# Hybrid decoder trunk: the sigmoid's table loaded early, the first low part behind the root, the third joint unit's first raw sum on VectorE, and the reloads of x two joint units later

## The chip, the cores and the metric

The kernel runs on one core of a Trainium2 chip. The metric is the device time of one execution in microseconds (us); where several runs are given, it is their median. The engines are called PE (matmuls), DVE (VectorE), ACT (ScalarE), POOL (GpSimd) and SP (SyncE, which here only starts DMAs).

## The reference

The trunk has two residual layers on a sequence of 1024 positions by 1024 channels, all in float32. Each layer is a token mixer and a SwiGLU network, each behind an RMSNorm and a modulation by a conditioning vector c:

```python
c_act = silu(c)
for i in range(2):
    sh_m, sc_m, g_m, sh_f, sc_f, g_f = split(c_act @ ada_w[i] + ada_b[i], 6)
    h = rms_norm(x, norm_mix_g[i]) * (1 + sc_m) + sh_m
    y = conformer_conv(h, ...) if i == 0 else multiscale_pool(h, ...)
    x = x + (1 + g_m) * y
    h = rms_norm(x, norm_ffn_g[i]) * (1 + sc_f) + sh_f
    x = x + (1 + g_f) * ((silu(h @ w_gate[i]) * (h @ w_up[i])) @ w_down[i])
return rms_norm(x, final_g)

def conformer_conv(h, ...):
    a, g = split(h @ w1 + b1, 2)
    u = a * sigmoid(g)
    u = silu(layer_norm(causal_depthwise_conv(u, width=31)))
    return u @ w2 + b2
```

The pooling mixer of layer 1 takes trailing means of 2, 4, 8 and 16 positions in four groups of channels, less the token itself, and maps each group linearly. The inner width of the SwiGLU network is 2816.

## The kernel before

**Number format.** A float32 product is made of three PE products in the type fp32r: each operand is split into a high part (a cast) and a low part (the operand less its high part), and high x high, high x low and low x high are summed. A weight tile `raw` (128 x 1024) thus costs a DMA (L473 in `load_weight`, L469), an ACT cast to the high part of `w`, and a subtraction on DVE or POOL for the low part, `w<-raw,w` in the profile. Activations are split in the same way into `h` high (ACT) and `h` low (DVE).

**Tiling.** Channels lie on the 128 partitions, in 8 tiles of channels. The sequence is cut into two chunks of 512 positions, A and B, so that a matmul is 128 x 128 by 128 x 512. Every engine's instruction is recorded at L122, a matmul at L144, and many of SP's DMAs at L154.

**Order of the work.** PE's order is written by hand: the order of the code. The other engines' orders come from a scheduler that works with estimated prices; where it would choose wrongly, the code ties an instruction behind another by an edge that is only an order and no semaphore (`add_manual_dep(..., edge, ...)`). `V_`, `S_` and `G_` issue on DVE, ACT and POOL. `either(n)` picks DVE or POOL.

**First stage (L1450 to L1525).** Chunk A's sums of squares go through PE; DVE works out the reciprocal root of their means in some ten small steps on 128 x 4 (`var`, `col`, in `rsqrt`, L496), and PE spreads it over the partitions (`rstd<-ident,col`). Beside it DVE multiplies tiles of the modulation weights by silu(c) and sums them (`ada_dot`; `adaw<-adaw,cact`), which gives shift and scale. Then for each of 8 channel tiles k, `t` is the normed and scaled x (DVE), `h` its split, and PE multiplies 8 banks (`first`) with weight tile k: 24 products a tile. The first two weight tiles' low parts are DVE's own (`own=k < 2`). When the last tile is through, ACT makes the sigmoid of the gate banks (`t<-first,vecs`), and the convolution's stage follows: the rest of the first matrix (`a`, `g`), the taps on DVE, POOL and ACT, and further modulation vectors by PE (`ada<-adaw,ccols`), whose weights come by SP (`adaw<-in_adan_dram`). ACT holds one function table at a time; its change is the row ACT_TABLE_LOAD.

**Joint units (L1080 to L1230, layer by layer).** In the SwiGLU network chunk A's first products are made ahead, and the two chunks' remaining products are put together by Strassen-like combinations: `joint(l, fp)` takes, for each of 11 pairs of inner channels `fp`, four quarters w0 to w3 of the gate and up weights and makes five weight tiles from sums of them, by `joint_weights`:

- `s2`: s = w0 + w3, and `s1`: w2, for the parts t2 (PE bank `a`) and t1 (PE bank `e`),
- `s3`: w0, `s4`: w1 + s (`raw<-raw,s` in the profile), `a22`: w3, for the parts n3 (`a`), b22 (`e`) and n4 (`a`).

Ahead of that, the quarters themselves are sums: `added(i, src)` (L1091) adds a quarter from memory onto a loaded one by an accumulating DMA of POOL's queue. For every fp but 0, w0 += w2 comes first and then w2 += w3. In layer 0's second unit (fp 1) the first of the two is a DVE addition instead. The name `raw<-in_wgu_dram` stands for loads and accumulations alike, `s<-raw,raw` for the sum s. When t1 is done, DVE takes the bank's two halves away by `t<-e,r`, and b22 writes into the same bank (`e<-b,w`), so PE waits for these two instructions. DVE prepares the next unit's weights while PE works on this one: `s<-raw,raw` and `t<-e,r` of two neighbouring units stand in one queue.

**Reloads.** The residual x of chunk A was stored to memory (`xd`) before and is taken back in four blocks during the joint units by `x_in(A, m)` (L331), an SP DMA `x<-xd` tied behind the last matmul of a unit. `all_joint` (L1648) runs the 11 units.

Of the kernel before, what the change touches and what calls it, by code (L numbers as in the profile page):

```python
# [9 lines left out]
F32 = mybir.dt.float32  # L10
# [6 lines left out]
P = 128  # L17
# [110 lines left out]
def trunk(ctx, tc, xT, c, vec, ada, adan, w1f, w1, wdg, w2, wgu, wdn, wpl, out):  # L128
# [232 lines left out]
    def V(name, j, n=1):  # L361
        b = _COLS[name] + j
        return vecs[:, b : b + n]
# [9 lines left out]
    def ada_dot(w, l, j, k):  # L373
        b = (l * 6 + j) * KT + k
        V_.scalar_tensor_tensor(w, w, 1.0, cact, op0=MUL, op1=MUL, accum_out=mod[:, b : b + 1])
# [711 lines left out]
    def joint_weights(l, fp):  # L1087

        w = {}

        def added(i, src):  # L1091
            d = order(nc.gpsimd.dma_start(w[i], wgu[l, fp, src], accum_op=ADD))  # L1092
            if fp == 1:
                st["added"].append(d.ins)
            clock["G"] = max(clock["G"], clock["PE"]) + 0.9

        def loads():
            for i in (0, 3, 2, 1) if fp else (2, 0, 3, 1):
                w[i] = quarter(l, fp, i, "u1")
            if fp == 1 and l == 0:  # L1100
                V_.tensor_tensor(w[0], w[0], w[2], op=ADD)
                if st["third"]:
                    tc.add_manual_dep(V_.last.ins, st["third"], edge, reason="behind the combinations")
                else:
                    st["early"].append(V_.last.ins)
            else:
                added(*((0, 2) if fp else (2, 3)))
            added(*((2, 3) if fp else (0, 2)))

        def later():  # L1110

            if fp == 1 and st["read"]:
                tc.add_manual_dep(V_.last.ins, st["read"], edge, reason="behind the first unit's reads")
            elif fp == 1:
                st["next"].append(V_.last.ins)

        def s2():
            if fp:
                loads()
            w[4] = block("u0", "s2", F32).rearrange("p a b -> p (a b)")  # L1120
            either(D).tensor_tensor(w[4], w[0], w[3], op=ADD)
            later()
            wt = combined(w[4])
            later()
            return wt

        def s1():
            if fp == 0:
                loads()
            wt = combined(w[2], fp == 0)  # L1130
            if fp:
                later()
            return wt

        def s3():
            wt = combined(w[0], fp == 0, True)
            later()
            return wt

        def s4():  # L1140
            either(D).tensor_tensor(w[1], w[1], w[4], op=ADD)
            return combined(w[1])

        def a22():
            wt = combined(w[3], fp == 0 and l == 0, True, wgu[l, fp, 3])
            if fp == 0 and l == 0:
                return wt
            if fp == 0 and st["third"]:
                tc.add_manual_dep(V_.last.ins, st["third"], edge, reason="behind the combinations")
            elif fp == 0:  # L1150
                st["early"].append(V_.last.ins)
            return wt

        return s2, s1, s3, s4, a22
# [319 lines left out]
    V_.scalar_tensor_tensor(acc, squares[KT - 1], EPS_SUM, acc, op0=ADD, op1=ADD)  # L1474
    summed = V_.last.ins.name
    S_.activation(ccols[:, :, 0], V("c", 0, KT), AF.Silu)
    scale_b = cst.tile([P, KT], F32, name="scale_b")
    G_.tensor_scalar(scale_b, V("ada_b", KT, KT), 1.0, None, op0=ADD)
    ada_m = ada.rearrange("(l j k) p d -> l k p j d", l=DEPTH, j=6)
# [14 lines left out]
    for k in range(KT + 1):  # L1494
# [14 lines left out]
                products(fb[q], wt, q, h_a[k - 1], k == 1, k == KT)  # L1509
        if k < KT:  # L1510
            ada_dot(w[:, 0], 0, 0, k)
            tc.add_manual_dep(V_.last.ins, low_last if k else rstd_last, edge, reason="behind the first norm")
            if k == 1:
                tc.add_manual_dep(dots[0], low_last, edge, reason="behind the first values")
            V_.tensor_scalar(scale_m[:, k : k + 1], mod[:, KT + k : KT + k + 1], scale_b[:, k : k + 1], V("norm_mix_g", k), op0=ADD, op1=MUL)
            V_.tensor_scalar(mod[:, k : k + 1], mod[:, k : k + 1], V("ada_b", k), None, op0=ADD)
            t = temp(A.n) if k else first_t
            V_.scalar_tensor_tensor(t, x[0][k], scale_m[:, k : k + 1], rstd_a if k else rstd_p, op0=MUL, op1=MUL)
            t_last = V_.last.ins.name
            S_.activation(h_a[k][0], t, AF.Identity, bias=mod[:, k : k + 1])  # L1520
            if k == 0:
                rstd_a = temp(A.n, "ny", 2)
                S_.copy(rstd_a, rstd_p)
            wt = load_weight(w1f[k], 2 * FIRST * P, load_next, own=k < 2)
    st["T"] = {}  # L1525
    for e in clock:
        clock[e] = max(clock.values())
# [123 lines left out]
    def all_joint(l, n, first=None, behind_it=None):  # L1651
# [6 lines left out]
        rest = [2 * q for q in range(ROUNDS[l] * ROUND, NP)] + list(range(1, NF, 2))  # L1658
        for fp in range(NP):
            joint(l, fp)  # L1660
            if 0 < fp <= KT // 2:
                unit(lambda take, m=fp - 1: x_in(A, m))
            if fp == 0:
                if first is not None:
                    first()
            if fp == NP - 2:
                unit(fetch(A, l, fours(rest)[0], "h1"))
# [115 lines left out]
```

## Time and profile before

| what | us |
|---|---|
| median of three runs | 1732.28 (1731.41 to 1732.43) |
| profiled execution | 1733.18 |
| its span in the trace | 1731.4 |
| PE busy | 1699.2 (98%) |
| DVE busy | 1300.0 (75%) |
| ACT busy | 788.8 (46%) |
| POOL busy | 464.6 (27%) |

The span is the time in which the trace has instructions; the profiled execution's own time is 1.8 us longer. A row of a timeline gives start, length, engine, line, operation, output and inputs (names without their numbers), shapes, count, and in brackets how long the engine had stood idle before it and what ended that. Rows that run together are joined (x24). A row of the table by stretches gives the length, then for each engine its busy time and count, the granted clock, the DMA engines' share and GB/s. PEld is PE's weight load, SPq is SP's queue. PE is pipelined, so the end of a matmul row is modelled, and neighbouring rows overlap a little. The sigmoid's table is loaded at 67.44 us.

### The profile page before, as it was taken

How to read it: one execution, taken by the hardware profiler on the slowest of the kernel's cores; microseconds unless marked ns; L12 is line 12 of the kernel's file. 1: busy time of each engine (PE TensorE's matmuls, PEld its weight loads, DVE VectorE, ACT ScalarE, POOL GpSimd, SP SyncE). 2: the span in 40 equal slices, each digit the busy share in tenths (PEclk: the TensorE clock that was granted, in tenths of full speed). 3: DMA queues.
4: the chain of work that ended last, by engine and by line, in shares of the span. 5: the costliest groups of instructions: out<-in, count | busy, mean ns of one | idle time of the engine just before them, and what ended most of it. 6: DMA issues, size and time to landing. Idle time of an engine off the chain costs nothing.

```text
span 1731.4 us, 21659 instructions
## 1 busy us (share of the span) xinstructions
PE 1699.2 (98%) x7746; PEld 1385.2 (80%) x7746; DVE 1300.0 (75%) x1878; ACT 788.8 (46%) x1080; POOL 464.6 (27%) x547
## 2 busy tenths in 40 slices
PE   6999999999999999999999999999999999999997
PEld 5777777778887788888888888888888888888887
DVE  7889898898669787887665987858776676555655
ACT  3669687876546232333223337457333333222213
POOL 2488867795001112221110301111111111000001
PEclk9999999999999999999999999999999999999999
DMA  7958987737775988977886837887777674655561
GB/s 278 300 169 219 243 224 201 212 104 208 244 231 138 289 281 277 289 244 261 312 277 210 268 112 222 238 292 193 233 240 230 174 216 145 256 207 207 173 230 60
DMA packets 111453, 385.44 MB, mean 223 GB/s; under 512 B 12145, under 2 KB 14321, under 8 KB 111346
## 3 DMA queue, kind: packets, MB, share of 16 engines
q1 hardware_dynamic: 74832, 256.11, 41.7%
q0 software_dynamic: 35424, 126.89, 29.5%
q8 instruction: 61, 1.00, 0.2%
q10 hardware_dynamic: 1090, 1.05, 0.2%
q14 instruction: 46, 0.38, 0.1%
HBM read 315.85 MB, written 63.96 MB: 219 GB/s over the span
## 4 chain that ended last, share of the span: by engine, by line
PE 84%; DVE 7%; DMA 3%; issue 2%; ACT 1%; POOL 1%; DVEq 0%; SPq 0%; ACTq 0%; POOLq 0%
PE dn L144 26%; PE a L144 21%; PE e L144 12%; PE p L144 11%; PE y L144 6%; PE g L144 3%; PE tap L144 2%; DMA raw<-in_wgu_dram 2%; DVE t L122 1%; DVE w L122 1%; POOL pa L122 1%; PE ada L144 1%; PE first L144 1%; DMA adaw<-in_adan_dram 1%; DVE adaw L122 1%
## 5 line engine op out<-in xcount | busy, mean ns | idle before, releaser
L122 ACT CAST w<-raw 128x1024 fp32r<-128x1024 f32 x269 | 281.9, 1050 | 498.0 <-PE dn L144 226.3
L144 PE MATMUL dn<-g,w 128*128 128x512 f32 (+1 forms) x2184 | 484.7, 383 | 1.7 <-DVE g L122 1.0
L144 PEld LDWEIGHTS dn<-g,w 128*128 128x128 f32 x2184 | 399.7, 188 | 82.2 <-DVE g L122 1.3
L122 DVE TENSOR_TENSOR w<-raw,w 128x1024 fp32r<-128x1024 f32 x197 | 244.5, 1244 | 70.5 <-ACT w L122 69.2
L144 PE MATMUL a<-n,w 128*128 128x512 f32 x1056 | 247.8, 390 | 1.1 <-DVE n L122 0.7
L144 PE MATMUL p<-h,w 128*128 128x512 f32 x1056 | 244.2, 390 | 0.8 <-DVE h L122 0.6
L122 POOL TENSOR_TENSOR pa<-pa,pr 128x512 f32<-128x512 f32 x160 | 229.7, 1517 | 23.1 <-ACT pr L122 20.0
L144 PEld LDWEIGHTS a<-n,w 128*128 128x128 f32 x1056 | 197.7, 188 | 44.4 <-DVE n L122 2.2
L144 PEld LDWEIGHTS p<-h,w 128*128 128x128 f32 x1056 | 197.2, 188 | 43.8 <-DVE h L122 1.5
L122 DVE SCALAR_TENSOR_TENSOR x<-dn,gains,x 128x512 f32<-128x512 f32 (+1 forms) x200 | 138.7, 726 | 96.8 <-PE dn L144 96.8
L122 DVE SCALAR_TENSOR_TENSOR ca<-u,vecs,ca 128x512 f32<-128x512 f32 x245 | 170.0, 747 | 0.5
L144 PE MATMUL e<-b,w 128*128 128x512 f32 x528 | 123.8, 390 | 2.1 <-DVE t L122 1.5
L144 PE MATMUL a<-t,w 128*128 128x512 f32 x528 | 123.9, 390 | 1.0 <-DVE w L122 1.0
L144 PE MATMUL e<-t,w 128*128 128x512 f32 x528 | 123.3, 389 | 0.0
L1092 POOL DMA_DIRECT2D raw<-in_wgu_dram x43 | 38.0, 885 | 306.7 <-DMA raw<-in_wgu_dram 112.4
L122 ACT ACTIVATE pr<-u,vecs 128x512 f32<-128x512 f32 x160 | 108.2, 716 | 25.2 <-POOL pa L122 19.8
L144 PEld LDWEIGHTS e<-b,w 128*128 128x128 f32 x528 | 98.9, 188 | 23.8 <-issue 1.4
L144 PEld LDWEIGHTS a<-t,w 128*128 128x128 f32 x528 | 98.9, 188 | 22.4 <-DVE w L122 1.9
L144 PEld LDWEIGHTS e<-t,w 128*128 128x128 f32 x528 | 99.1, 188 | 20.6
L161 POOL DMA_DIRECT2D gd<-g x76 | 47.6, 629 | 177.0 <-DVE g L122 176.8
L144 PE MATMUL y<-v,w 128*128 128x512 f32 x384 | 89.3, 391 | 0.5 <-DVE v L122 0.5
L144 PEld LDWEIGHTS y<-v,w 128*128 128x128 f32 x384 | 71.5, 188 | 17.6 <-issue 1.6
(164 smaller groups left out, 1970.1 us busy)
## 6 DMA issues: line engine op xcount, KB each, us to landing
raw<-in_wgu_dram SPq DMA_DIRECT2D x132, 512.0 KB, 4.8
raw<-in_wdn_dram SPq DMA_DIRECT2D x88, 512.0 KB, 7.0
gd<-g POOLq DMA_DIRECT2D x76, 512.0 KB, 7.2
g<-gd SPq DMA_DIRECT2D x76, 512.0 KB, 5.7
adaw<-in_ada_dram POOLq DMA_DIRECT2D x48, 512.0 KB, 7.2
raw<-in_wgu_dram POOLq DMA_DIRECT2D x43, 512.0 KB, 7.1
raw<-in_w_dram SPq DMA_DIRECT2D x36, 512.0 KB, 6.6
adaw<-in_adan_dram SPq DMA_DIRECT2D x32, 512.0 KB, 5.5
```

Of the source, the lines that this page charges most:

```text
L122: self.last = self.order(getattr(self.eng, name)(out, *args, **kw))
L144: last_mm[0] = nc.tensor.matmul(out, lhsT, rhs, start=start, stop=stop, skip_group_check=more).ins.name
L161: return order(nc.gpsimd.dma_start(*a))
L1092: d = order(nc.gpsimd.dma_start(w[i], wgu[l, fp, src], accum_op=ADD))
```

## The change

Four edits; all matmuls and their order stay as they are.

```diff
@@ joint_weights, loads()
-            if fp == 1 and l == 0:
+            if fp == 2:
+                V_.tensor_tensor(w[0], w[0], w[2], op=ADD)
+            elif fp == 1 and l == 0:
                 V_.tensor_tensor(w[0], w[0], w[2], op=ADD)
@@ first stage
     S_.activation(ccols[:, :, 0], V("c", 0, KT), AF.Silu)
+    silu = S_.last.ins.name
+    S_.activation(tmp.tile([P, 16], F32, tag="col0", name="second_act", bufs=1)[:, 0:1], ones[:, 0:1], AF.Sigmoid)
+    tc.add_manual_dep(S_.last.ins, silu, edge, reason="the sigmoid's table early")
...
             ada_dot(w[:, 0], 0, 0, k)
+            dot2 = V_.last.ins.name
             tc.add_manual_dep(V_.last.ins, low_last if k else rstd_last, edge, reason="behind the first norm")
...
             wt = load_weight(w1f[k], 2 * FIRST * P, load_next, own=k < 2)
+            if k == 0:
+                tc.add_manual_dep(V_.last.ins, dot2, edge, reason="behind the root")
@@ all_joint
-            if 0 < fp <= KT // 2:
-                unit(lambda take, m=fp - 1: x_in(A, m))
+            if 2 < fp <= 2 + KT // 2:
+                unit(lambda take, m=fp - 3: x_in(A, m))
```

- A dummy sigmoid on one column stands behind ACT's silu of `ccols`, so that the sigmoid's table is loaded there.
- The low part of the first weight tile is tied behind the first tile's `ada_dot` (both on DVE), which itself is tied behind the reciprocal root.
- In the third joint unit (fp 2) of both layers, w0 += w2 is a DVE addition of 128 x 1024 instead of an accumulating DMA; the second sum, w2 += w3, stays an accumulating DMA and must now wait until DVE has read w2.
- The four reloads of x stand behind the fourth to the seventh joint unit instead of the second to the fifth, in both layers.

How the order moves, in three places. The first is DVE in the first norm, before. `var`, `col` are the root's small steps, `w_323` the first weight tile, `w_362` the second, `t_297` and `h_298` belong to channel tile 0:

```order
L122 TENSOR_TENSOR var_278<-var_278,col_283 128x4
L122 TENSOR_TENSOR w_323<-raw_321,w_323 128x1024
L122 SCALAR_TENSOR_TENSOR var_278<-var_278,col_283 128x4
L122 SCALAR_TENSOR_TENSOR col_283<-var_278,col_283 128x4
L122 SCALAR_TENSOR_TENSOR adaw_275,mod<-adaw_275,cact 128x1024
L122 TENSOR_SCALAR mod<-mod,vecs 128x1
L122 SCALAR_TENSOR_TENSOR t_297<-x_79,gains,rstd_292 128x512
L122 TENSOR_TENSOR w_362<-raw_360,w_362 128x1024
L122 SCALAR_TENSOR_TENSOR h_298<-t_297,mod,h_298 128x512
```

The same place now (all numbers are two higher: `w_325` is the first weight tile, `w_364` the second):

```order
L122 TENSOR_TENSOR var_280<-var_280,col_285 128x4
L122 SCALAR_TENSOR_TENSOR var_280<-var_280,col_285 128x4
L122 SCALAR_TENSOR_TENSOR col_285<-var_280,col_285 128x4
L122 SCALAR_TENSOR_TENSOR adaw_277,mod<-adaw_277,cact 128x1024
L122 TENSOR_TENSOR w_325<-raw_323,w_325 128x1024
L122 TENSOR_SCALAR mod<-mod,vecs 128x1
L122 SCALAR_TENSOR_TENSOR t_299<-x_79,gains,rstd_294 128x512
L122 SCALAR_TENSOR_TENSOR h_300<-t_299,mod,h_300 128x512
L122 SCALAR_TENSOR_TENSOR adaw_328,mod<-adaw_328,cact 128x1024 x2
L122 TENSOR_TENSOR w_364<-raw_362,w_364 128x1024
```

The first low part has moved from the middle of the root to a place behind `adaw`, and the second from ahead of the low half `h` to a place behind two further `adaw` rows.

The second place is ACT at the end of the first stage, before. `first_307` and `first_309` are gate banks, `w_662` and `w_672` weight tiles of the convolution's stage:

```order
L122 ACTIVATE h_305<-t_591,mod 128x512
L122 CAST w_631<-raw_629 128x1024
L122 CAST w_662<-raw_660 128x1024
L122 ACTIVATE w_662<-raw_660 128x1024
L122 ACT_TABLE_LOAD
L122 ACTIVATE t_640<-first_307,vecs 128x512
L122 CAST w_672<-raw_670 128x1024
L122 ACTIVATE w_672<-raw_670 128x1024
L122 ACTIVATE t_645<-first_309,vecs 128x512
```

The same place now:

```order
L122 ACTIVATE h_307<-t_593,mod 128x512
L122 CAST w_633<-raw_631 128x1024
L122 ACTIVATE t_642<-first_309,vecs 128x512
L122 ACTIVATE t_647<-first_311,vecs 128x512
L122 CAST w_664<-raw_662 128x1024
L122 ACTIVATE w_664<-raw_662 128x1024
L122 ACTIVATE acc_705<-x_83 128x512
L122 ACTIVATE t_653<-first_313,vecs 128x512
```

The table load is gone from here (it stands behind `ccols`, ahead of ACT's first CAST), and two sigmoids have moved ahead of the two passes on `w_664`. On SP's queue, the third of the loads `adaw<-in_adan_dram` has moved ahead of one weight load of the convolution's stage.

The third place is DVE where layer 0's second unit meets the weights of the third, before. `t_5073` and `t_5087` empty the second unit's bank `e`, `s_800_5054` is the third unit's sum s, `raw_5044` to `raw_5050` its quarters:

```order
L122 TENSOR_TENSOR t_5073<-e_5059,r_790_5010 128x512
L122 TENSOR_TENSOR g_5003<-t_5000,g_5003 128x512
L122 TENSOR_TENSOR s_800_5054<-raw_5044,raw_5046 128x1024
L122 TENSOR_TENSOR t_5087<-e_5060,r_791_5011 128x512
L122 TENSOR_TENSOR raw_5050<-raw_5050,s_800_5054 128x1024
L122 TENSOR_TENSOR w_5056<-s_800_5054,w_5056 128x1024
```

The same place now:

```order
L122 TENSOR_TENSOR t_5075<-e_5061,r_790_5012 128x512
L122 TENSOR_TENSOR g_5005<-t_5002,g_5005 128x512
L122 TENSOR_TENSOR raw_5046<-raw_5046,raw_5050 128x1024
L122 TENSOR_TENSOR s_800_5056<-raw_5046,raw_5048 128x1024
L122 TENSOR_TENSOR t_5089<-e_5062,r_791_5013 128x512
L122 TENSOR_TENSOR raw_5052<-raw_5052,s_800_5056 128x1024
L122 TENSOR_TENSOR w_5058<-s_800_5056,w_5058 128x1024
```

The addition of two quarters is new, between the second unit's two `t<-e,r`. In the fourth unit's weights one `t<-e,r` now stands ahead of `raw<-raw,s`, where both stood behind it.

## The prediction

> **What bounds the kernel now.** I read the page's busy times first, then the view of the waits of the matmul engine (PE), then timelines around each of its stops. From the page:
>
> ```profile
> span 1731.4 us, 21659 instructions
> ...
> PE 1699.2 (98%) x7746; PEld 1385.2 (80%) x7746; DVE 1300.0 (75%) x1878; ACT 788.8 (46%) x1080; POOL 464.6 (27%) x547
> ```
>
> PE is busy for 98% of the span, and the change leaves every matmul in place, so it can only work on the time in which PE stands or runs slowly. The stops that it can reach are bracketed in the rows below: `rstd` and `first` (part 1), `a` (part 2), `ada` (behind it), `e` (part 3). VectorE (DVE, 75%) and ScalarE (ACT, 46%) have room on the whole, so what they are given costs only where it stands ahead of something that PE waits for.
>
> **Part 1: the first weight tile's low part.** DVE, then PE, in the first norm:
>
> ```profile
> 15.50 0.17 DVE L122 TENSOR_TENSOR var<-var,col 128x4 f32<-128x4 f32 x1
> 15.58 1.23 DVE L122 TENSOR_TENSOR w<-raw,w 128x1024 fp32r<-128x1024 f32 x1
> 16.72 0.16 DVE L122 SCALAR_TENSOR_TENSOR var<-var,col 128x4 f32<-128x4 f32 x1
> 16.92 0.16 DVE L122 SCALAR_TENSOR_TENSOR col<-var,col 128x4 f32<-128x4 f32 x1
> 17.00 1.22 DVE L122 SCALAR_TENSOR_TENSOR adaw<-adaw,cact 128x1024 f32<-128x1024 f32 x1
> ...
> 19.31 0.76 DVE L122 SCALAR_TENSOR_TENSOR t<-x,gains,rstd 128x512 f32<-128x512 f32 x1 [0.84 <-PE rstd L144]
> 19.98 1.22 DVE L122 TENSOR_TENSOR w<-raw,w 128x1024 fp32r<-128x1024 f32 x1
> ```
>
> ```profile
> 17.23 2.05 PE L144 MATMUL rstd<-ident,col 128*128 128x128 f32 x8 [3.07 <-DVE col L122]
> 20.84 0.79 PE L144 MATMUL first<-h,w 128*128 128x512 f32 x1 [1.57 <-ACT h L122]
> ```
>
> The low part (15.58, 1.23 us) sits in the middle of the reciprocal root, whose steps otherwise follow each other every 0.20 us (16.72 to 16.92). Without it the step of 16.72 starts at 15.50 + 0.20 = 15.70: `col`, and PE's `rstd` behind it, come 1.02 us sooner, so `rstd` ends at 18.26 instead of 19.28. Now the low part stands behind `adaw`, which starts at 17.00 − 1.02 = 15.98 and ends near 17.20; it ends at 18.4, and with the small step on `mod` behind it (about 0.1) `t` starts at 18.45 instead of 19.31: 0.86 us sooner, and the first product with it, at 19.98. The second product needs the low half of `h`, which stood behind the second tile's low part (19.98, 1.22) and now precedes it. It follows ACT's high half, which moves by those 0.86 us, so it comes at least as much sooner. The term is thus 0.86 at its least, 1.15 if the second product gains what its queue lost; I take 1.0. The second tile's low part now stands behind two `adaw` products, some 2.4 us; PE needs it only behind the 24 products of the first tile, so it costs nothing as long as these last, 5.44 us even at the full rate. If that cover were gone, 2.4 us would be lost.
>
> **Part 2: the sigmoid's table.** ACT, then PE, at the end of the first stage:
>
> ```profile
> 67.44 1.28 ACT L122 ACT_TABLE_LOAD   x1
> ```
>
> ```profile
> 69.48 5.73 PE L144 MATMUL a<-h,w 128*128 128x512 f32 x24 [1.14 <-ACT t L122]
> ```
>
> PE is through with `first` at 69.48 − 1.14 = 68.34 and stands 1.14 us for a sigmoid that waited for its table. In the new order the table is loaded right behind `ccols`, ahead of ACT's first cast, and the first two sigmoids stand ahead of two weight passes. The gate bank that the first sigmoid reads closes early in PE's last stretch, so it can run before 68.34, and the stop goes. Besides its idle time a stop costs a slow restart, 5.73 against 5.60 us for 24 matmuls (rows of PE in part 3), 0.13; and the overlap with the group behind: undisturbed groups of 5.60 follow each other after 5.44 (706.00 to 711.44 there), 0.16. The stop is worth 1.14 + 0.13 + 0.16 = 1.43. It would be worth 0 if that bank closed last. The dummy itself (about 0.2 us, and the table's 1.28) lies in ACT's idle time ahead of its first cast:
>
> ```profile
> 14.46 1.04 ACT L122 CAST w<-raw 128x1024 fp32r<-128x1024 f32 x1 [3.12 <-DMA raw<-in_w1f_dram]
> ```
>
> 1.5 us go into 3.12; without that cover they would delay the cast, and with it the low part of part 1, by up to 1.5.
>
> **What of parts 1 and 2 comes through.** Wanted are 1.0 + 1.43 = 2.4 us of lead. Behind them lies the convolution's start:
>
> ```profile
> 80.00:90.00 10.00, 9.08 (x51) 6.30 (x50) 10.00 (x17) 8.96 (x14) 7.15 (x7) 1.00 1.06 283
> ```
>
> ```profile
> 82.08 0.33 SPq L154 DMA_DIRECT2D adaw<-in_adan_dram  x1
> ```
>
> ```profile
> adaw<-in_adan_dram SPq DMA_DIRECT2D x1, 512.0 KB, 11.9
> ```
>
> ```profile
> 88.61 0.64 PE L144 MATMUL ada<-adaw,ccols 128*32 128x256 f32 x8 [0.92 <-DMA adaw<-in_adan_dram]
> 89.18 5.76 PE L144 MATMUL g<-h,w 128*128 128x512 f32 x24
> 94.87 0.64 PE L144 MATMUL ada<-adaw,ccols 128*32 128x256 f32 x8
> ```
>
> In this stretch the DMA engines' share (next to last column) is 1.06: full, and PE already stands 0.92 for an `adaw`. The next one is issued at 82.08 and lands 11.9 us later, at 93.98, 0.89 before PE wants it at 94.87. A faster PE makes that load late unless its issue moves too. The issues follow buffers that PE and ACT release, so I let them move by part 1's 1.0 us, but not by part 2's, since full queues hand out no more. Then PE's lead at 94.87 is at most 1.0 + 0.89 = 1.9 us. I count **1.9**; the least is 0.9 (transfers don't move at all), the most 3.3 (both terms and the stop of 0.92 as well, if the loads come early: the third of them now stands one place further up SyncE's queue). Past some 230 us nothing in the order changes until the joint units, and PE's stops there wait on engines that wait on PE, so a lead is carried.
>
> **Part 3: the joint units of layer 0.** DVE, then PE, with one reload from SyncE's queue:
>
> ```profile
> 574.67 1.23 DVE L122 TENSOR_TENSOR s<-raw,raw 128x1024 f32<-128x1024 f32 x1 [7.68 <-DMA raw<-in_wgu_dram]
> ...
> 600.54 1.23 DVE L122 TENSOR_TENSOR raw<-raw,s 128x1024 f32<-128x1024 f32 x1 [2.90 <-DMA raw<-in_wgu_dram]
> ...
> 681.59 1.23 DVE L122 TENSOR_TENSOR raw<-raw,s 128x1024 f32<-128x1024 f32 x1 [3.32 <-DMA raw<-in_wgu_dram]
> ...
> 706.16 1.23 DVE L122 TENSOR_TENSOR raw<-raw,s 128x1024 f32<-128x1024 f32 x1 [2.35 <-DMA raw<-in_wgu_dram]
> ```
>
> ```profile
> 576.55 3.01 PE L144 MATMUL e<-b,w 128*128 128x512 f32 x12 [0.49 <-DVE t L122]
> ...
> 602.52 5.72 PE L144 MATMUL e<-b,w 128*128 128x512 f32 x24 [0.96 <-DVE t L122]
> ...
> 684.24 5.60 PE L144 MATMUL e<-b,w 128*128 128x512 f32 x24
> ...
> 706.00 5.60 PE L144 MATMUL a<-n,w 128*128 128x512 f32 x24
> 711.44 4.92 PE L144 MATMUL e<-b,w 128*128 128x512 f32 x21
> ```
>
> ```profile
> 582.74 0.38 SPq L154 DMA_DIRECT2D x<-xd  x1
> ```
>
> At 574.67 DVE has stood 7.68 us for the accumulating DMA of the third unit's first sum, with the second unit's `t<-e,r` queued behind it; PE stops 0.49. With the sum on DVE (1.23 us, inside those 7.68) only plain loads are waited for, and the stop goes: 0.49 + 0.13 + 0.16 = 0.78. At 600.54 DVE stands 2.90 for a raw load that shared the queue with the reload of `x` issued at 582.74; PE stops 0.96. With the reload two units later and one `t<-e,r` ahead of that step, this goes too: 0.96 + 0.12 + 0.16 = 1.24. Together **2.0**; at least 0.3 (another stop of nearly that size), at most 2.3. The price of moving the sum is that the second accumulating DMA overwrites a tile that DVE must have read first, so it starts about when DVE's sum ends rather than with the loads; a low part hangs on it. I put it at nothing, since it is one sum of 1.23 later; the bound is one stop, 1.24. In layer 1 the trace shows no stop of that kind, so I count no gain there.
>
> The reloads now fall into the windows of the fifth to the eighth unit; the fifth and sixth (681.59) had one before too. What PE needs is that DVE's step starts 602.52 − 600.54 = 1.98 ahead of it. In the sixth unit's window, with a reload, it starts 684.24 − 681.59 = 2.65 ahead: margin 0.67. In the seventh's, without one, 711.44 − 706.16 = 5.28 ahead: margin 3.30. A reload so eats some 2.6, and one that is new in the seventh window leaves about 0.7: I count 0. The bound is a stop as long as that of the third unit in each of the two new windows, 2 x 1.24.
>
> **Sum.** −1.9 − 2.0 = −3.9. Against the profiled execution's 1733.18 that gives 1729.3; that execution lies 0.9 over the median, 1732.28, so the forecast is **1728.4**. About 0.2% (3.5 us, that is below 1728.8 or above 1735.7) is what a measurement of this kernel can tell from no change.
>
> **The rivals.**
>
> *The slow start ends one step sooner.* Equal stretches of PE at its start, both busy throughout:
>
> ```profile
> 24.26:27.68 3.42, 3.42 (x10) 2.65 (x9) 3.42 (x4) 0.72 (x1) 2.11 (x1) 1.00 0.70 199
> 27.68:31.10 3.42, 3.42 (x17) 2.81 (x16) 3.42 (x9) 0.22 (x1) 0.00 (x0) 1.00 0.66 264
> ```
>
> Ten matmuls, then seventeen (two of each are cut by the ends): PE runs at about half rate until 27.7, though the granted clock (third column from the end) reads 1.00 in both. If the rate goes up at a fixed step of such a grid once PE has filled a stretch, a start 0.86 us sooner can fill the stretch from 20.84 to 24.26, and the full rate comes 3.42 us sooner: 15 matmuls in place of 8 there, 7 x 0.23 = 1.6 us beyond the sum. That gives 1728.4 − 1.6 = 1726.8. For it: the first products come at 19.98, ahead of that stretch. Against it: its gap between first and second product may stay, and the grid falls differently in each execution. The Trainium skill, "TensorE: Matmul & The Clock Gate", "Part 1: The HAM clock gate (the "warmup" mystery)", states this rule: half rate by default, full rate after one busy window of about 3.4 us, and windows that run freely and don't start with the kernel. By that rule the sum would be −5.5 in the phase of this trace, and near −3.9 in most others; the counts of 10 and 17 agree with it. Chance 0.11.
>
> *The convolution's start swallows the lead.* The loads don't move up, only 0.89 + 2.0 = 2.9 come through: 1729.4. For it: the DMA share of 1.06, and 11.9 us to landing. Chance 0.14.
>
> *The joint units' stops stay*, because DVE's combination then waits for the raw loads themselves, or the late accumulation stops PE in their place: 1732.28 − 1.9 = 1730.4. For it: the 2.90 at 600.54 was for a plain load. Chance 0.11.
>
> *The change does nothing on PE's path:* each gain is followed by a wait on the same transfers; 1732.3. Chance 0.03.
>
> *Slower: the moved reloads stop PE.* In the windows of units 5 to 8 a reload makes the raw load late, DVE's `raw<-raw,s` holds back `t<-e,r`, and PE stops as at 602.52, 1.24 each: 4 units x 2 layers x 1.24 = 9.9, less 3.9: 1738.3. It decides where that step starts more than 0.67 us later, measured against PE, than at 681.59. For it: that small margin, and a DVE that has a sum more to do. Against it: in that very window there was a reload before, and nothing stopped. Chance 0.08.
>
> **How the numbers follow.** The forecast's case has 0.53; its own range is 1727.4 to 1729.4, of which 0.39 lie below 1728.8 and 0.14 above. Faster by over 0.2%: 0.39 + 0.11 = 0.50. Within it: 0.14 + 0.14 + 0.11 + 0.03 = 0.42. Slower: 0.08. The range goes from the sooner full rate to the stops that stay, with a little on each side for the unknown costs: 1726.6 to 1730.8; outside are the slow case, the case of no effect and the edges of the others.
>
> **What would show it.** In the profile after, the root's steps should follow each other without `w`, `t` at about 18.5 and the first product at about 20.0; a table load before ACT's first cast and none at 67; `a<-h,w` without a wait for ACT; an `ada` stop near 93 that is about as long as before or longer, not gone; `s<-raw,raw` of the third unit about 3 us earlier; no stop of `e` in the second and third unit; none in units 5 to 8. The prediction is wrong if PE's stops in `first` or `e` keep their lengths, if a new stop over 1 us appears in the joint units or before 110 us, or if a lead seen at 95 us is gone at 560 us.

## The result, and the profile after

| | median | runs | from | to |
|---|---|---|---|---|
| before | 1732.19 us | 21 | 1730.53 | 1734.51 |
| changed | 1729.34 us | 21 | 1728.48 | 1731.94 |

The ratio is 0.9986, with a 95% interval of 0.998 to 0.9992: 2.85 us faster by the medians, which is 0.16% and so less than the 0.2% that the prediction held to be distinguishable. Forecast were 1728.4 us and a range of 1726.6 to 1730.8. The profiled execution of the changed kernel took 1731.56 us (span 1729.7), 2.2 above its median; the rows below show a stretch at half rate that is worth 1.6 of that. One execution of "reloads alone" below took 6148.93 us at a granted clock of 0.345 and is left out of its median and ratio.

The first norm, DVE and then PE, as in the prediction's first two fences:

```profile
15.23 0.17 DVE L122 TENSOR_TENSOR var<-var,col 128x4 f32<-128x4 f32 x1
15.43 0.17 DVE L122 SCALAR_TENSOR_TENSOR var<-var,col 128x4 f32<-128x4 f32 x1
15.63 0.16 DVE L122 SCALAR_TENSOR_TENSOR col<-var,col 128x4 f32<-128x4 f32 x1
...
16.86 1.22 DVE L122 TENSOR_TENSOR w<-raw,w 128x1024 fp32r<-128x1024 f32 x1
...
18.12 0.74 DVE L122 SCALAR_TENSOR_TENSOR t<-x,gains,rstd 128x512 f32<-128x512 f32 x1
```

```profile
15.94 2.04 PE L144 MATMUL rstd<-ident,col 128*128 128x128 f32 x8 [1.85 <-DVE col L122]
19.64 25.59 PE L144 MATMUL first<-h,w 128*128 128x512 f32 x98 [1.65 <-ACT h L122]
```

The root's steps now follow every 0.20 us, `rstd` starts 1.29 sooner, the first product 1.20, and the second one has no wait in this view: its row is part of the x98. `t` has no bracket: what it waits for is DVE's own low part, as the prediction had it.

ACT in the same stage and at its end:

```profile
10.98 1.28 ACT L122 ACT_TABLE_LOAD   x1
...
14.09 1.04 ACT L122 CAST w<-raw 128x1024 fp32r<-128x1024 f32 x1 [1.61 <-DMA raw<-in_w1f_dram]
...
62.56 0.69 ACT L122 ACTIVATE t<-first,vecs 128x512 f32<-128x512 f32 x1 [1.60 <-PE first L144]
```

The dummy and its table lie in idle time (1.61 of it are left), and the first sigmoid runs at 62.56, almost 4 us before PE needs it. PE at the convolution's start, which is where the gain is given back:

```profile
66.44 5.60 PE L144 MATMUL a<-h,w 128*128 128x512 f32 x24
...
84.45 0.64 PE L144 MATMUL ada<-adaw,ccols 128*32 128x256 f32 x8
...
92.08 0.64 PE L144 MATMUL ada<-adaw,ccols 128*32 128x256 f32 x8 [1.31 <-DMA adaw<-in_adan_dram]
...
93.56 7.32 PE L144 MATMUL a<-h,w 128*128 128x512 f32 x24
100.81 0.64 PE L144 MATMUL ada<-adaw,ccols 128*32 128x256 f32 x8
```

```profile
90.60:94.00 3.40, 2.09 (x19) 1.47 (x19) 2.80 (x7) 3.22 (x5) 3.40 (x4) 1.00 1.06 372
94.00:97.50 3.50, 3.50 (x11) 2.72 (x10) 3.50 (x8) 2.74 (x5) 3.50 (x4) 0.52 1.03 305
```

`a` starts without a wait, 3.04 sooner than before; the third ada group has lost its stop of 0.92 and is 4.16 ahead; the fourth stops 1.31 and is 2.79 ahead. Then the group of 24 takes 7.32 instead of 5.60 to 5.74, with no wait inside: in 94.00 to 97.50 the granted clock (third column from the end) is 0.52. PE is set to half rate for about 3.4 us, from 2.0 us behind the end of the stop. At 100.81 only 1.16 are left, and this lead is carried almost unchanged to the joint units (536.05 against 537.18).

The joint units of layer 0, DVE and PE:

```profile
569.35 1.23 DVE L122 TENSOR_TENSOR raw<-raw,raw 128x1024 f32<-128x1024 f32 x1 [3.12 <-DMA raw<-in_wgu_dram]
570.61 1.22 DVE L122 TENSOR_TENSOR s<-raw,raw 128x1024 f32<-128x1024 f32 x1
```

```profile
572.10 5.60 PE L144 MATMUL e<-b,w 128*128 128x512 f32 x24
...
599.30 5.60 PE L144 MATMUL e<-b,w 128*128 128x512 f32 x24
...
708.59 5.72 PE L144 MATMUL e<-b,w 128*128 128x512 f32 x24 [0.33 <-DVE t L122]
```

Both stops of `e` are gone (the sum s is at 570.61 instead of 574.67), and a small one, 0.33, has come in the seventh unit, whose window has a reload now.

### The profile page after: what moved, and what is told of

Same layout as the page of the kernel before. It is cut to its first block, busy times and chain, and to the rows that moved or that the text cites. A ratio compares the mean times of both kernels' runs of the same rounds, so it can differ in the third digit from the quotient of the medians.

```text
span 1729.7 us, 21674 instructions
## 1 busy us (share of the span) xinstructions
PE 1699.9 (98%) x7746; PEld 1386.6 (80%) x7746; DVE 1304.3 (75%) x1880; ACT 787.3 (46%) x1081; POOL 460.8 (27%) x545
## 4 chain that ended last, share of the span: by engine, by line
PE 86%; DVE 6%; DMA 3%; issue 2%; ACT 1%; POOL 1%; SPq 0%; DVEq 0%; ACTq 0%; POOLq 0%
PE dn L144 26%; PE a L144 21%; PE e L144 12%; PE p L144 11%; PE y L144 6%; PE g L144 3%; PE first L144 3%; PE tap L144 2%; DMA raw<-in_wgu_dram 1%; DVE t L122 1%; POOL pa L122 1%; PE ada L144 1%; DMA adaw<-in_adan_dram 1%; DVE w L122 1%; PE var L144 1%
```

## The experiments

Medians in us; each row's kernel before was run beside it on the same chip, since the medians of the kernel before differ by up to 1.3 from one such group to another. The ratio is not exactly the quotient of the two medians.

| kernel | median (runs) | before (runs) | ratio, 95% interval |
|---|---|---|---|
| sigmoid alone | 1731.76 (11) | 1732.04 (35) | 1.0001, 0.9993 to 1.001 |
| low part alone | 1732.01 (11) | 1732.04 (35) | 1.0002, 0.9993 to 1.001 |
| sum on DVE alone | 1731.09 (11) | 1732.04 (35) | 0.9995, 0.9987 to 1.0004 |
| reloads alone | 1732.44 (11) | 1732.04 (35) | 1.0004, 0.9995 to 1.0012 |
| changed, ada later | 1729.01 (9) | 1733.36 (31) | 0.9974, 0.9965 to 0.9984 |
| changed, reloads as before | 1729.52 (11) | 1733.36 (31) | 0.998, 0.9971 to 0.9988 |
| sigmoid and low part | 1731.65 (11) | 1733.36 (31) | 0.999, 0.9982 to 0.9999 |
| changed, stop filled | 1730.12 (11) | 1733.36 (31) | 0.9983, 0.9974 to 0.9992 |
| changed, again | 1730.23 (11) | 1732.17 (33) | 0.9986, 0.9977 to 0.9995 |
| ada later, again | 1731.06 (11) | 1732.17 (33) | 0.9991, 0.9982 to 1.0 |
| ada later, reloads as before | 1730.58 (11) | 1732.17 (33) | 0.9993, 0.9984 to 1.0002 |
| ada later, bias behind | 1728.52 (11) | 1732.17 (33) | 0.9981, 0.9972 to 0.999 |

**Sigmoid alone.** The kernel before with

```diff
     S_.activation(ccols[:, :, 0], V("c", 0, KT), AF.Silu)
+    silu = S_.last.ins.name
+    S_.activation(... name="second_act" ..., ones[:, 0:1], AF.Sigmoid)
+    tc.add_manual_dep(S_.last.ins, silu, edge, reason="the sigmoid's table early")
```

> The kernel before with the first edit alone (dummy sigmoid behind silu). Both theories: no table load near 67, the stop of a<-h,w (1.14) is gone, PE some 1.4 us ahead of the kernel before at its third ada group. Theory 1, the loads of adaw cap the lead: an ada stop behind it grows, PE is at most 0.9 ahead at the fifth ada group (101.97 before), time -0.9 or less. Theory 2, the loads move up with PE and what costs is a stretch at half rate (eight matmuls of 0.43 instead of 0.23, 1.6 us) behind an ada stop that meets the short var group: where this trace shows no such stretch the lead of 1.4 stays at 101.97, time about -1.4; where it does, PE is even or behind there.

The stop of `a<-h,w` went. ACT at this place, before and then in this run:

```profile
65.42 1.05 ACT L122 CAST w<-raw 128x1024 fp32r<-128x1024 f32 x1 [2.75 <-DMA raw<-in_w_dram]
66.37 1.05 ACT L122 ACTIVATE w<-raw 128x1024 fp32r<-128x1024 f32 x1
67.44 1.28 ACT L122 ACT_TABLE_LOAD   x1
68.74 0.69 ACT L122 ACTIVATE t<-first,vecs 128x512 f32<-128x512 f32 x1
```

```profile
62.98 1.05 ACT L122 CAST w<-raw 128x1024 fp32r<-128x1024 f32 x1 [2.46 <-DMA raw<-in_w_dram]
63.93 1.06 ACT L122 ACTIVATE w<-raw 128x1024 fp32r<-128x1024 f32 x1
64.89 0.67 ACT L122 ACTIVATE t<-first,vecs 128x512 f32<-128x512 f32 x1
```

The sigmoid still stands behind the two passes on a weight tile, which wait for their load; only the table's load ahead of it is gone. PE stood at the third ada group instead:

```profile
85.93 0.64 PE L144 MATMUL ada<-adaw,ccols 128*32 128x256 f32 x8 [1.65 <-DMA adaw<-in_adan_dram]
```

1.65 in place of the 0.92 of the kernel before, and no stretch at half rate there. Counted from the `var` groups PE is 1.9 ahead of the kernel before at the fifth ada group (the table in the next section), which is the second theory's case, but no gain in time could be measured.

**Low part alone.** The kernel before with

```diff
             ada_dot(w[:, 0], 0, 0, k)
+            dot2 = V_.last.ins.name
...
             wt = load_weight(w1f[k], 2 * FIRST * P, load_next, own=k < 2)
+            if k == 0:
+                tc.add_manual_dep(V_.last.ins, dot2, edge, reason="behind the root")
```

> The kernel before with the second edit alone (first low part behind the root). Both theories: first product 0.9 to 1.2 us sooner, no 0.28 wait of the second product, 1.0 to 1.5 ahead when the stage of first ends; the stop for the sigmoid stays near 1.1. Theory 1 (the adaw loads cap the lead): at most 0.9 to 1.0 ahead at 101.97, time -1.0. Theory 2 (only a half-rate stretch takes the lead back): 1.2 to 1.5 ahead there, time -1.3, unless the granted clock shows a stretch near 0.5 between 85 and 100. If the full rate also comes a step sooner in the first stage: 1.7 more.

Against every expectation the sigmoid's stop went with this edit too. ACT, and then PE:

```profile
60.72 1.28 ACT L122 ACT_TABLE_LOAD   x1
62.31 0.69 ACT L122 ACTIVATE t<-first,vecs 128x512 f32<-128x512 f32 x1 [0.31 <-PE first L144]
```

```profile
66.19 5.60 PE L144 MATMUL a<-h,w 128*128 128x512 f32 x24
...
92.29 0.64 PE L144 MATMUL ada<-adaw,ccols 128*32 128x256 f32 x8 [1.77 <-DMA adaw<-in_adan_dram]
...
94.01 7.10 PE L144 MATMUL a<-h,w 128*128 128x512 f32 x24
```

The table is still loaded late, but the scheduler now puts it and the sigmoid ahead of the two passes on a weight tile, where ACT is idle. At the fourth ada group stand the stop, and the slow group of 7.10 behind it, as in the changed kernel. The time did not change. The third joint unit stops for 2.06 here (602.54) where the kernel before had 0.96, with the same code in that place: this stop varies between executions.

**Sum on DVE alone.** The kernel before with

```diff
-            if fp == 1 and l == 0:
+            if fp == 2:
+                V_.tensor_tensor(w[0], w[0], w[2], op=ADD)
+            elif fp == 1 and l == 0:
                 V_.tensor_tensor(w[0], w[0], w[2], op=ADD)
```

> The kernel before with the third edit alone (third joint unit's first sum on DVE, both layers). If the accumulating DMA was what stopped PE at 576.55: that stop (0.49) goes, the one at 602.52 (0.96), which waits for a plain load beside a reload of x, stays: time -0.8. If the sum's move also sets the loads of the fourth unit free sooner: both go, -2.0. If it only shifts the stop to the late second accumulation: 0. In layer 1 nothing in any case.

```profile
598.55 5.60 PE L144 MATMUL e<-b,w 128*128 128x512 f32 x24
...
626.17 5.73 PE L144 MATMUL e<-b,w 128*128 128x512 f32 x24 [0.25 <-DVE t L122]
```

```profile
595.68 0.68 DVE L122 TENSOR_TENSOR t<-e,r 128x512 f32<-128x512 f32 x1
598.30 1.23 DVE L122 TENSOR_TENSOR raw<-raw,s 128x1024 f32<-128x1024 f32 x1 [1.94 <-DMA raw<-in_wgu_dram]
```

Both stops went (in the second unit `e` starts at 571.08 without a wait), although a reload of x still went beside the raw loads, and 0.25 came in the fourth unit. The order of `t<-e,r` ahead of `raw<-raw,s` came with this edit too: DVE still waits 1.94 for the raw load at 598.30, but the first half of bank `e` is free before that. Of the three expectations the second held in the trace; the time, 0.95 lower, is not clear of no change.

**Reloads alone.** The kernel before with

```diff
-            if 0 < fp <= KT // 2:
-                unit(lambda take, m=fp - 1: x_in(A, m))
+            if 2 < fp <= 2 + KT // 2:
+                unit(lambda take, m=fp - 3: x_in(A, m))
```

> The kernel before with the fourth edit alone (reloads of x two units later). If the reload behind the second unit was what made the raw load of 600.54 late: the stop of 602.52 goes and that of 576.55 (0.49) stays, a stop of 0.3 as in the changed kernel appears near 710: 1.24 less about 0.6, time -0.6. If the new stop near 710 comes from the moved sum and not from the reload: no stop there, time -1.2. If the reloads cost the same wherever they lie: a stop near 1.0 in one of the later units, time 0.

DVE, PE and the table by stretches in the third unit:

```profile
601.76 1.23 DVE L122 TENSOR_TENSOR raw<-raw,s 128x1024 f32<-128x1024 f32 x1 [4.36 <-DMA raw<-in_wgu_dram]
```

```profile
603.73 7.35 PE L144 MATMUL e<-b,w 128*128 128x512 f32 x24 [2.09 <-DVE t L122]
```

```profile
600.50:604.00 3.50, 1.41 (x7) 0.90 (x6) 2.24 (x3) 0.00 (x0) 0.26 (x1) 1.00 1.01 220
...
605.20:608.60 3.40, 3.40 (x9) 2.63 (x8) 3.23 (x6) 1.45 (x3) 0.53 (x1) 0.51 0.78 273
```

None of the three expectations held as a whole: without a reload in this window DVE waits 4.36 for the raw load instead of 2.90, PE stops 2.09, and the half rate comes here as well, behind a stop in quite another stage. The reload was not what made that load late. The small stop near 710 did not come.

**Ada later.** The changed kernel, with the fourth ada group and those behind it one group of PE's work later:

```diff
-LOAD = {"load": 4.0, "slow": 6.0, "next": 4.0, "dots": 4.0}
+LOAD = {"load": 4.0, "slow": 6.0, "next": 4.0, "dots": 4.0, "late": 9.0}
...
-            yield "load"
+            yield "late" if (j, k) == (2, 3) else "load"
```

> The changed kernel with the fourth ada group (and those behind it) one group of 24 matmuls later in PE's order, nothing else. Theory 1 (the loads of adaw near 92 cap what the first two edits bring): the stop of 1.31 goes, since its load has 5.4 us more, the lead of PE at the fifth a group is 3 to 4 us instead of 1.2 to 2.8, time 1 to 2 us below the changed kernel. Theory 2 (the half-rate stretch behind that stop is what costs): the stretch goes with the stop, and no execution shows it, time 0.5 to 1.5 below, most at the long end of the spread. Theory 3 (the full DMA queues cap the whole stage): a stop of 1 to 2 us appears at the next weight tile or ada group, time as the changed kernel's.

In its trace the stop and the half rate at 92 went, but a stop of 1.21 came at 155.13, where `a<-h,w` waits for a sigmoid on ACT, and one of 0.77 at 179.59 for an `adaw`. The ratio of 0.9974 looks like a better kernel; "ada later, again" below has the same kernel a second time.

**Reloads as before.** The changed kernel with the fourth edit undone (the diff of "reloads alone" turned round).

> The changed kernel with the reloads of x behind the second to fifth unit again (fourth edit undone). If the reload's move is what frees the third unit: the stop near 600 is back with 0.5 to 2, time +1 to +2 against the changed kernel. If the sum on DVE alone frees it (as with the third edit alone, where it was gone): no stop near 600, and none near 709, time 0 to -0.6.

```profile
597.49 5.60 PE L144 MATMUL e<-b,w 128*128 128x512 f32 x24
```

No stop of `e` near 600: the sum on DVE frees the third unit without the fourth edit. Two small stops stand beside it, 0.36 at 591.92 and 0.45 at 625.30. At the fourth ada group this execution stopped 1.01, with no half rate behind it:

```profile
91.24 0.64 PE L144 MATMUL ada<-adaw,ccols 128*32 128x256 f32 x8 [1.01 <-DMA adaw<-in_adan_dram]
...
92.72 5.71 PE L144 MATMUL a<-h,w 128*128 128x512 f32 x24
```

**Sigmoid and low part.** The kernel before with the first two edits together.

> The changed kernel with the third and fourth edit undone: sigmoid and first low part alone. If the gains of single edits add up (-0.3 and 0.0 measured alone): -0.3 against the kernel before. If each alone is eaten by the ada loads and both together too: the stop near 92 between 1 and 2, lead at 102 us about 1, time -1. If the lead passes where no half-rate stretch follows: lead 2.4 to 2.8 at 102 us, time about -1.5 to -2. In the joint units the stops of 0.5 and 1 to 2 are as before.

```profile
91.45 0.64 PE L144 MATMUL ada<-adaw,ccols 128*32 128x256 f32 x8 [1.38 <-DMA adaw<-in_adan_dram]
...
92.94 7.31 PE L144 MATMUL a<-h,w 128*128 128x512 f32 x24
```

1.7 us by the medians, with an interval of about 0.2 to 3.1, so some gain passes. Stop and slow group are there again; the joint units' stops (0.53 and 0.81) stay, as expected.

**Stop filled.** The changed kernel with twelve matmuls by zeros ahead of the fourth ada group, which leave the sums as they are:

```diff
+            if (j, k) == (2, 3):
+                for _ in range(12):
+                    nc.tensor.matmul(acc[:, :Q], zeros, st["h", 0][0][0][:, :Q], start=False, stop=False, ...)
             for g in range(4):
                 matmul(acc[32 * g : 32 * g + 32, :Q], ...)
```

> The changed kernel with twelve added matmuls of 128x256 (zeros, added to the ada bank) ahead of the fourth ada group, about 1.4 us, as long as its stop. If low use of PE around that stop is what sets it to half rate: no half-rate stretch near 94, and the long executions (1731 and more) go; median 0.3 to 0.6 below the changed kernel. If the stretch has another cause (the time itself, the load on DMA): it comes as often as before, and the median is the same or up to 1.4 above.

```profile
90.03 1.58 PE L443 MATMUL ada<-h,zeros 128*128 128x256 f32 x12
91.54 0.64 PE L144 MATMUL ada<-adaw,ccols 128*32 128x256 f32 x8
...
93.02 5.73 PE L144 MATMUL a<-h,w 128*128 128x512 f32 x24
```

No stop, no half rate, and PE is where it is with the stop (79.90 us behind the `var` group, against 79.85). That fits the low use of PE as the cause, but one trace without a half rate proves little, since with the reloads as before there was none behind a stop of 1.01 either. By time it is not decided: of 11 executions three still took over 1731, and the interval is nearly the changed kernel's. This trace also has a stop of 0.59 at 168.57, for an `adaw`, and one of 0.64 at 579.54 in the second joint unit, where `a<-n,w` waits for DVE's `t`, in code that is the changed kernel's.

**Changed, again.** The changed kernel itself.

> The changed kernel itself once more, beside the three below on one chip. If the half-rate stretch behind the fourth ada group hangs on where a free grid falls, a new execution shows it or not, as a matter of chance; the stop of 1.0 to 1.4 at that group is there in any case, and PE is 2.4 to 3 ahead of the kernel before at 102 us without the stretch and about 1.2 with it. Median 2 to 3 below the kernel before.

A stop of 1.09 at the fourth group, a slow group of 7.24 behind it, and no stop of `e` behind the first joint unit, the seventh included. The ratio, 0.9986, is that of the first measurement.

**Ada later, again.** The kernel of "ada later".

> The changed kernel with the ada groups one group of matmuls later from the fourth on, a second time. If the cap at the fourth group was worth what its stop and its half-rate stretch cost: 1.0 to 1.6 below the changed kernel of the same chip, no stretch near 94, the stop of 1.2 at 155 (a sigmoid that stands behind the bias additions of x on ACT) as in its first trace. If that advantage was the chip's and not the kernel's: within 0.5 of the changed kernel.

```profile
181.82 0.64 PE L144 MATMUL ada<-adaw,ccols 128*32 128x256 f32 x8 [2.48 <-DMA adaw<-in_adan_dram]
182.39 7.37 PE L144 MATMUL tap<-us,w 128*128 128x512 f32 x24
```

The advantage did not repeat: 0.83 above the changed kernel of the same chip. The stop for the sigmoid is there again (1.54 at 155.66); the wait for an `adaw`, now at 181.82, is longer and has the half rate behind it.

**Ada later, reloads as before.** The same kernel with the fourth edit undone.

> The same with the reloads of x behind the second to fifth unit again. If the fourth edit is worth nothing by itself beside the sum on DVE: within 0.5 of the run above, stops of 0.3 to 0.5 near 592 and 625 in place of one near 709. If it is worth what the third unit's stop cost: 1.2 above it, with a stop near 600.

Within 0.5 of the kernel above, and no stop of `e` behind the first joint unit in its trace, nor the stops near 155 and 180, though its code is the same there. By the times the fourth edit shows no worth of its own.

**Ada later, bias behind.** The kernel with later ada groups, and in `biased`, for chunk A,

```diff
+            if ch.i == 0:
+                tc.add_manual_dep(S_.last.ins, st["mark"], edge, reason="behind the inputs")
```

where `st["mark"]` is the last matmul of the inputs' products.

> The kernel with later ada groups, and chunk A's bias additions of x on ACT tied behind the last input product of that stage (about 165 us). If these additions in front of the sigmoid make the stop of 1.2 at 155: it goes, and the time is 1.0 to 1.4 below that kernel's. If the sigmoid waits for something else: the stop stays, time the same. If ACT is then late further on: a new stop between 165 and 250.

The stop at 155 went. That fits the additions as its cause but does not show it, since "ada later, reloads as before" has no such stop either, without this edit. The DMA's stop stayed, with the half rate behind it:

```profile
167.82 0.64 PE L144 MATMUL ada<-adaw,ccols 128*32 128x256 f32 x8 [1.82 <-DMA adaw<-in_adan_dram]
168.39 7.33 PE L144 MATMUL tap<-us,w 128*128 128x512 f32 x24
```

This has the lowest median of the four kernels run beside each other, 1728.52 against 1730.23 of the changed kernel. The intervals against the kernel before overlap, so it is the best candidate and not a shown improvement.

## Why the prediction was right, and where it was not

The median moved the way that was forecast and lies in the range; the forecast of −3.9 us was 1 us too much. The traces say where the microsecond is. Two lengths can be read in each: from the start of the first `var` group, which no edit touches, to `e<-b,w` of the first joint unit (537.18 before), and from there to the long row of `dn<-g,w` behind the joint units (965.95 before). The first is taken without the edits from the kernel before, sum alone and reloads alone, and with them from the five traces marked "both" below; the second without them from the kernel before, sigmoid alone, low part alone and both of these, and with them from both traces of the changed kernel, the filled stop and the three with later ada groups and later reloads. Means in us, with their ranges:

| length | without the edits that touch it | with them | gained | forecast |
|---|---|---|---|---|
| `var` to the joint units | 523.97 (3 traces, 522.99 to 524.89) | 523.25 (5, 521.90 to 523.85) | 0.7 | 1.9 |
| joint units to `dn` | 428.93 (4, 428.48 to 429.76) | 426.86 (6, 426.44 to 427.51) | 2.1 | 2.0 |

Together 2.8, where the medians show 2.85; these few traces would allow a wider difference. The joint units' term is clear of the spread and as forecast; the first stage's was about a third of the forecast, in ranges that overlap. By the prediction's steps:

**The gain up to `a` was sized right on average, but the two terms were not the worth of two edits.** The start of the span differs between executions by more than these terms, so the traces are compared from the same `var` group. Starts of PE's groups, in us behind it:

| trace | `a<-h,w` | fourth ada | fifth ada |
|---|---|---|---|
| old first stage: before | 57.19 | 82.58 | 89.68 |
| old: sum alone | 55.51 | 79.90 | 87.01 |
| old: reloads alone | 57.27 | 81.66 | 88.76 |
| sigmoid alone | 54.48 | 80.63 | 87.77 |
| low part alone | 54.22 | 80.32 | 89.07 |
| both edits: changed | 54.21 | 79.85 | 88.58 |
| both: changed, again | 54.30 | 79.72 | 88.42 |
| both: reloads as before | 54.24 | 79.57 | 86.69 |
| both: sigmoid and low part | 54.21 | 79.90 | 88.63 |
| both: stop filled | 54.22 | 79.90 | 87.04 |

At `a` the mean of the old three is 56.66, that of the new five 54.24: 2.4 sooner, which is what the prediction wanted from parts 1 and 2. The old three differ by 1.8 among themselves, so the closeness is in part luck. Each edit alone is there too: 54.48 and 54.22. The stop of 1.14 was rightly charged to the table: with the sigmoid alone the table's load is all that is gone from ACT's order at this place, and the stop went, while sum alone, whose weight load landed about as early behind `var`, still stopped 0.65. But with the low part alone the table is still loaded late, and the stop went as well, since load and sigmoid there stand ahead of the two weight passes. Either edit takes away the same stop, so neither term is what its edit is worth: beside the low part the early table adds nothing here.

**Part 1's lead did not pass through `first` as a lead.** The prediction took DVE's 75% as room. In this stage DVE is nearly full, as the trace with the reloads as before shows:

```profile
50.38 2.57 DVE L122 SCALAR_TENSOR_TENSOR t<-x,gains,ny 128x512 f32<-128x512 f32 x1
...
56.13 2.57 DVE L122 SCALAR_TENSOR_TENSOR t<-x,gains,ny 128x512 f32<-128x512 f32 x1
```

```profile
30.00:66.00 36.00, 35.98 (x155) 28.27 (x154) 33.47 (x47) 14.17 (x18) 17.83 (x6) 1.00 0.82 293
```

DVE (third busy time, 33.47 of 36.00) takes 5.75 us for each channel tile, 2.57 of them for `t` (0.74 for the first tile's), and PE's 24 products take 5.44. With the low part behind the root the first low half of `h` is done 8.1 to 8.3 us behind `var`, instead of 9.4 to 9.6, but the third comes at 20.1 to 20.4 in all fourteen traces, and the eighth at 48.8 to 49.1 in all but that of the kernel before (50.47). PE's second product of a tile needs that half. So in all ten traces with this edit the last product of `first` starts 53.98 to 54.19 us behind `var`, however early PE was; in the four without it, at 54.26, 54.48, 55.32 and 55.66, mean 54.93, in the order in which their full rate began (12.9, 13.5, 15.2 and 15.4). The forecast 1.0 came as 0.9 on average, but as the difference between an end that DVE fixes and one that hangs on the slow start.

**The cap by the `adaw` loads was the right mechanism, with a wrong detail.** At the fourth ada group the means are 81.38 and 79.79: 1.6 of the 2.4 are left, where the prediction counted 1.9; one of the old three (sum alone) is as early as the new ones here. The detail: the load's issue was to move by 1.0 only; it moved by 3.2, from 82.08 to 78.91, with PE's ada group ahead of it, and the landing time grew instead, from 11.9 to 13.1. This also is where each edit alone lost its lead: at stops of 1.65 with the sigmoid and 1.77 with the low part. That both together passed something by the times (0.999) and neither alone did isn't explained by the traces, and the intervals overlap.

**What failed was the step from there on: that a lead past the fourth group is carried.** Behind the stop there PE is set to half rate in some executions, and at the fifth group the three new traces with it (changed, changed again, sigmoid and low part) average 88.54, no better than the old 88.48, while the two without it average 86.87. Eight matmuls at about 0.43 instead of 0.227 are 1.6 us, as much as the whole lead. The prediction knew the half rate only at the start of the kernel. The mean of all five is 0.6 ahead there, and 0.7 at the joint units: from the fifth group on the lead is carried, as forecast. Of the timed executions the mean granted clock is on record. The seven traces without such a stretch read 0.997 or 0.998, the seven with one 0.996 or 0.997. Of the changed kernel's 21 executions four read 0.996 and took 1730.48 to 1731.94 us, and five read 0.998 and took 1728.48 to 1729.83; the twelve at 0.997 are undecided. Of 99 executions of the kernel before in the experiments one reads 0.996. So the half rate seems more frequent in the changed kernel and goes with its long executions; its exact part in the missing 1.0 us stays open. The Trainium skill, "TensorE: Matmul & The Clock Gate", "Part 1: The HAM clock gate (the "warmup" mystery)", gives the half rate after an idle window of about 3.4 us. The length agrees (0.52 over 94.00 to 97.50, where the trace's own record has 3.41 us at 0.5); but the stretch ahead was not idle, PE was busy for 2.09 of 3.40 us in it.

**The joint units were sized right, for a wrong reason in one half.** The change took both stops, of 0.49 and 0.96, and brought one of 0.33 in its first trace and none in the second. Restart and lost overlap included that is 2.0 less 0.6 and 2.0; the forecast was 2.0, and the lengths above give 2.1. But the second stop was put down to the reload issued at 582.74. Without that reload the stop was 2.09, and with it, but the sum on DVE, there was none. The step that failed reads a raw load as late because of its neighbour in the queue; what the sum on DVE did in its place was to let DVE go through the third unit's quarters sooner and to put one `t<-e,r`, for which PE waits, ahead of the step that waits for the load. Of the 2.1 the sum brings 1.6: the three traces with it and the reloads as before have 426.93, 427.23 and 427.95, mean 427.37. The last 0.5 would be the reloads', in ranges that overlap.

**The rivals.** That the convolution's start swallows the lead was the nearest to the result by its place and by its number, 1729.4. That number is luck: its condition was that the loads don't move up, and they moved by 3.2. The slow start's sooner end did happen in single executions, but was not worth what the rival said. The same stretch in the changed kernel and with the reloads as before:

```profile
20.84:24.26 3.42, 3.42 (x9) 2.64 (x9) 3.42 (x8) 0.17 (x1) 0.00 (x0) 1.00 0.17 29
```

```profile
20.84:24.26 3.42, 3.42 (x13) 2.72 (x12) 3.42 (x9) 0.03 (x1) 0.00 (x0) 1.00 0.23 54
```

Nine matmuls there, thirteen here, and yet both come to `a` at 54.2 behind `var`: what is won at the start is given back to DVE's pace by the end of `first`. The slower rival did not come: in the windows of the fifth to the eighth unit there was one stop of `e`, of 0.33, in the first trace of the changed kernel and none in the second.

## What to carry to other kernels

A lead given to the busiest engine is worth what passes the next engine that is full in that stage, whatever its share of the whole, and the next full queue: look for the first transfer behind it whose landing is close to its use, and expect edits that each remove the same wait not to add up. Where a stop varies between executions (0.81 to 2.06 us here, in the same code), one trace doesn't tell its cause; undo the suspected cause alone. And a stop's price is not its length: where PE's use is low around it, a slow stretch behind it can cost as much again.

## What the runs showed of the hardware

PE was set to half rate not only at the start: stretches at 0.51 to 0.53 of the clock, about 3.4 us long, began 0.8 to 2.1 us behind the end of stops of 1.09, 1.31, 1.38, 1.77, 1.82, 2.09 and 2.48 us, in three different stages, and did not come behind stops of 1.01, 1.14, 1.21, 1.54, 1.57, 1.65 and 2.06. So the length of the stop alone doesn't decide. In the clock records of these seven traces the stretch is 3.413 us long each time and begins a whole number of 3.413 us behind the moment at which the full rate first came: 20 in four of them, 43, 46 and 169 in the others. So it falls on a fixed grid, and a stop can lie across two of its cells, as that of 1.01 did. What decides within a cell stays open: in the cell ahead PE was busy for 0.9 to 2.3 us of 3.41 where the half rate followed, and for 1.8 around the stops of 1.65 and 2.06, where it did not.

In the first stage the clock column reads 1.00 while matmuls follow every 0.43 us instead of 0.23, so there the rate is read from the matmuls: the first record of the clock begins only where the full rate does, at 27.70 us before and at 25.84 in the changed kernel's trace.
